# The second mixer's opening: products on the unscaled stream, keys and ctx norm behind them

## The chip, the cores and the metric

The kernel runs on one core of a Trainium2 chip. The metric is the device time of one execution in microseconds (us). The engines are PE (matrix products), DVE and ACT (element by element), POOL, and SP, whose queue issues most of the DMAs.

## The reference

A network of two blocks at batch 1, on 512 tokens of width 1024. The first block has two mixer layers; the first of them also updates a context of 256 tokens, which the second one reads for keys and values. The lines that matter:

```python
h = rms_norm(x, norm_g) * (1 + scale[:, None]) + shift[:, None]
hc = rms_norm(ctx, norm_g) * (1 + scale_c) + shift_c
p = h @ w_in                    # a_in, b_in (pool), q, k, v, gate
pkv = hc @ w_in[:, K_OFF:G_OFF] # layer 1: keys and values of the context
y = jnp.concatenate([fourier_mix(a_in, w_fourier), pool_mix(b_in, w_pool, pool_scale), attn], axis=-1)
x_new = x + gate[:, None] * ((y * jax.nn.silu(g)) @ w_out)
```

`scale`, `shift` and `gate` are products of one vector with large matrices (the modulations). The second block has, twice, a hybrid mixer (a retention and an HGRN2 part, a gate, an out projection) and a convolutional feed-forward part, each with modulations of its own.

## The kernel before

Activations lie transposed: a tile is 128 features by 512 tokens, eight tiles make the stream `x`, and ctx tiles have 256 columns. Each operand is kept as a high and a low part: a weight tile of 128x1024 is split by ACT (`wh`, L151) and DVE (`wl`, L152), and each product is three matmuls (L178 to L180, where 512 tokens of the activations move; L201 to L203 for keys and values, where the activations are loaded and 256 columns of the weight move). A product of one weight tile with all eight tiles of the stream is thus 24 matmuls of 512 columns. Weights are streamed through two buffers by SP in the order of the array `w_in`, whose column tiles the host lays out in the order of use.

A list scheduler sets the order of every engine, except in `pinned(...)` stretches, where the written order stands. PE, DVE, ACT and POOL each run their order strictly. Background work, the modulations of later layers, is handed to the scheduler by `background(n)`: `n` steps, each a DMA of 256 KB into one of two buffers `gr` and a product on DVE with a broadcast vector `cb` (`gemv`, L515). `background(99)` takes what is left; `mod_finish` and `gain` (L519 to L525) then make the modulation usable. A new vector `cb` is itself a DMA, three ACT steps and a DVE product (`bcast_silu`, L500).

The places that are spoken of below:

- **The junction of mixer 0 and mixer 1** (about 405 to 480 us). Before, `cross_first` (L415) handles it: the last two tiles of the out projection are made in halves of 256 tokens, so that the norm of the first half can begin early; the norm (`norm_mix`, L269) is shared by DVE, ACT and POOL, and PE's first products of mixer 1 are the keys of both halves and a pool projection on the normed stream. The context's norm follows, on the same engines.
- **The other junctions** use `cross` (L305). PE goes on with three products on A*x, the stream times the modulation's gain but without the division by the norm ("deferred" tiles). Meanwhile the norm's factor r is found (a statistic on PE, `rstd` on ACT and DVE). A deferred tile is finished by `z(j)`: its sum in PSUM times r, plus a bias, which PE makes from the shift vector (`bias_rows` L309, `bias_cols`, `bias_pick`). `first(k)` and `second(k)` (L374, L378) make the normed stream for all later products: DVE multiplies by gain and r, ACT adds the shift and writes `hh`, DVE writes the low part `hl`.
- **Mixer 1's tail** (about 655 to 680 us): the last attention head, the gates, and then the out projection.
- **The first hybrid mixer's end** (about 860 to 1005 us), called ssm0: four retention heads, eight gate tiles (product on PE, silu, product with `y` L1621, split into `y2h` and `y2l`), and the out projection, whose residual is L1054.

Of the kernel before, what the change touches and what calls it, by code (L numbers as in the profile page):

```python
# [12 lines left out]
F32 = mybir.dt.float32  # L13
# [7 lines left out]
P = 128  # L21
# [15 lines left out]
def tile_model(ctx: ExitStack, tc: tile.TileContext, a: dict, out: bass.AP, dbg=None):  # L37
# [191 lines left out]
    def stat_add(i, xk, k, sl, eng=None, late=None):  # L229
        n = sl.stop - sl.start  # L230
        if k == 0:
            acc[i] = sb("acc", [P, T], F32, 1, cp) if i == 0 else sb("acc2", [P, C], F32, 1, sub[0])
            act(acc[i][:, sl], xk[:, sl], AF.Square)
            return None
# [70 lines left out]
    def cross(load, steps, res, per, hs, A, sh, swap=None):  # L305
        d0 = wi[0] + KT * per
        b = {}

        def bias_rows(j):  # L309
            if not b:  # L310
                b["pick"] = tmp("rs", 1)
                V.tensor_reduce(out=b["pick"], in_=ident.rearrange("p (g c) -> p c g", g=4)[:, 0:1], op=ALU.add, axis=AX.X)
                b["sh"] = tmp("t", KT * 32).rearrange("p (k c) -> p k c", c=32)
# [8 lines left out]
        def bias_cols():  # L322
            rows = tmp("t", ND * P)
            act(rows, b["ps"][:, :ND * P], AF.Copy)
            b["rows"] = rows

        def bias_pick():
            o = b["ps"][:, ND * P:ND * P + ND]
            for j in range(ND):
                PE.matmul(o[:, j:j + 1], b["rows"][:, j * P:(j + 1) * P], b["pick"], start=True, stop=True, skip_group_check=True)  # L330
            b["col"] = tmp("rs", ND)
# [8 lines left out]
        for m in range(KT - 1):  # L340
# [4 lines left out]
            pre(m)  # L345
        with pinned(PE_, DVE_, ACT_, POOL_):
# [6 lines left out]
            bias_rows(2)  # L353
            bias_cols()
            run(st[-4:])
            bias_pick()
            last = res(m, o, ALL)
            pre(m)
            V.tensor_tensor(out=acc[0], in0=acc[0], in1=last, op=ALU.add)
            if swap is not None:  # L360
                swap()
            zs, ts, os_ = [], {}, []

            def defer(n):
                w = next_w(n)
                os_.append(pt("g"))
                return gemm_steps(os_[-1], w, hs)

            def z(j):
                zs.append(tmp("t"))  # L370
# [3 lines left out]
            def first(k):  # L374
                ts[k] = tmp("ta" if k % 4 < 3 else "t")
# [6 lines left out]

            st = defer(2)
            run(st[:5])
            sq = pt("m")
            PE.matmul(sq, ones, acc[0], start=True, stop=True)
            run(st[5:])
            r = rstd(sq, T, 1.0 / D, "ta", tmp("t"))
            run(defer(1))
# [8 lines left out]
            first(3)  # L398
            second(1)
            z(1)  # L400
# [10 lines left out]
            z(2)  # L411
        anchor.update(tails(DVE_, ACT_))
        return zs

    def cross_first(load, steps, res, full, stat_c, hs, hc, mods_, k_steps, p_steps, weights):  # L415
        (Ax, mx), (Ac, mc) = mods_
        for m in range(KT - 2):
            w = load(m, 2)
            o = pt("g")
            run(steps(o, w, ALL))  # L420
            res(m, o, ALL)
            full(m, w)
        with pinned(PE_, DVE_, ACT_, POOL_):
            tail = [(m, load(m, KT - m), pt("g")) for m in range(KT - 2, KT)]
            for m, w, o in tail:
                run(steps(o, w, HA))
                last = res(m, o, HA)
            sq = pt("m", C)
            stat(sq, acc[0][:, HA], True)
            rest = [f for m, w, o in tail for f in steps(o, w, HB)]  # L430
            run(rest[:3])
            stat(sq, last, False)
            ra = stat_rstd(sq)
            run(rest[3:])
            lasts, adds, halves, rs_ = [], [], [], {}

            def res_b(j):
                m, w, o = tail[j]
                lasts.append(res(m, o, HB, adds))

            def take():
                halves.clear()
                W.load(wi[0] + 2)
                W.split(wi[0] + 1, halves)
                if halves:
                    halves[0]()
                weights.append(next_w(0))

            def late_half():
                if len(halves) > 1:  # L450
                    halves[1]()

            def stat_b():
# [1407 lines left out]
```

## Time and profile before

| | |
|---|---|
| median of 3 runs | 2064.59 us (2062.36 to 2070.71) |
| profiled execution | 2064.29 us, its span 2062.5 us, mean granted PE clock 0.993 |
| busy | PE 2007.8 us (97%), DVE 1418.3 (69%), ACT 945.2 (46%), POOL 120.1 (6%) |
| weight splits | DVE 338.4 us in 279 instructions, ACT 291.0 us |
| background products (L515) | DVE 208.9 us in 304 instructions |

Times in the rows are counted from the start of the span; 1.79 us of the execution lie outside it. PE's records overlap (a 512-column matmul shows 0.39 us but the next starts 0.23 us later), so its pace is read from starts. The granted clock (PEclk) is a share of 2.4 GHz.

### The profile page before, as it was taken

How to read it: one execution, taken by the hardware profiler on the slowest of the kernel's cores; microseconds unless marked ns; L12 is line 12 of the kernel's file. 1: busy time of each engine (PE TensorE's matmuls, PEld its weight loads, DVE VectorE, ACT ScalarE, POOL GpSimd, SP SyncE). 2: the span in 40 equal slices, each digit the busy share in tenths (PEclk: the TensorE clock that was granted, in tenths of full speed). 3: DMA queues.
4: the chain of work that ended last, by engine and by line, in shares of the span. 5: the costliest groups of instructions: out<-in, count | busy, mean ns of one | idle time of the engine just before them, and what ended most of it. 6: DMA issues, size and time to landing. Idle time of an engine off the chain costs nothing. (4 is left out here: it accounts for less than half of the span.)

```text
span 2062.5 us, 30076 instructions
## 1 busy us (share of the span) xinstructions
PE 2007.8 (97%) x11398; PEld 1718.6 (83%) x11398; DVE 1418.3 (69%) x2722; ACT 945.2 (46%) x1629; POOL 120.1 (6%) x129
## 2 busy tenths in 40 slices
PE   7999999989999999999999999999999999999997
PEld 4988988889898888888788888878988888888887
DVE  4879997686676688888787776338986667444323
ACT  4527487253547455435453333225643645333322
POOL 2101010130101100000100000000000010000010
PEclk9999999999999999999999999999999999999999
DMA  8342325724012332355446665323122223333332
GB/s 295 108 148 63 116 64 157 244 79 150 22 52 67 118 112 72 103 173 181 159 149 214 207 208 181 99 88 101 52 72 82 82 84 104 101 92 102 88 101 77
DMA packets 96129, 245.92 MB, mean 119 GB/s; under 512 B 12592, under 2 KB 17952, under 8 KB 95728
## 3 DMA queue, kind: packets, MB, share of 16 engines
q1 hardware_dynamic: 94752, 242.90, 37.3%
q8 instruction: 90, 1.47, 0.3%
q0 software_dynamic: 656, 0.57, 0.1%
q10 hardware_dynamic: 576, 0.52, 0.1%
q14 instruction: 55, 0.45, 0.1%
HBM read 239.76 MB, written 4.19 MB: 118 GB/s over the span
## 5 line engine op out<-in xcount | busy, mean ns | idle before, releaser
L152 DVE TENSOR_TENSOR wl<-wr,wh 128x1024 fp32r<-128x1024 f32 (+1 forms) x279 | 338.4, 1213 | 238.2 <-ACT wh L151 234.9
L178 PE MATMUL g<-hh,wh 128*128 128x512 f32 (+1 forms) x1256 | 493.1, 393 | 0.0
L180 PE MATMUL g<-hh,wl 128*128 128x512 f32 (+1 forms) x1256 | 491.1, 392 | 1.3 <-DVE wl L152 1.1
L179 PE MATMUL g<-hl,wh 128*128 128x512 f32 (+1 forms) x1256 | 492.0, 392 | 0.0
L151 ACT ACTIVATE wh<-wr 128x1024 fp32r<-128x1024 f32 (+1 forms) x279 | 291.0, 1043 | 384.9 <-PE g L179 302.7
L515 DVE SCALAR_TENSOR_TENSOR gs<-gr,cb 128x512 bf16<-128x512 f32 x304 | 208.9, 687 | 99.6 <-DMA gr<-ada_w 80.0
L180 PEld LDWEIGHTS g<-hh,wl 128*128 128x128 f32 x1256 | 236.2, 188 | 47.6 <-DVE wl L152 1.3
L179 PEld LDWEIGHTS g<-hl,wh 128*128 128x128 f32 x1256 | 236.5, 188 | 47.1 <-DVE hl L381 1.2
L178 PEld LDWEIGHTS g<-hh,wh 128*128 128x128 f32 x1256 | 236.5, 188 | 45.8 <-issue 1.0
L201 PE MATMUL g<-wh,hh 128*128 128x256 f32 x704 | 203.6, 290 | 3.6 <-ACT hh L661 3.1
L202 PE MATMUL g<-wl,hh 128*128 128x256 f32 x704 | 203.9, 290 | 2.3 <-DVE wl L152 2.3
L203 PE MATMUL g<-wh,hl 128*128 128x256 f32 x704 | 202.7, 289 | 2.2 <-DVE hl L295 2.1
L201 PEld LDWEIGHTS g<-wh,hh 128*128 128x128 f32 x704 | 136.6, 194 | 6.9 <-ACT hh L661 3.4
L178 PE MATMUL g<-g2h,wh 128*128 128x512 f32 (+1 forms) x374 | 141.9, 379 | 0.0
L179 PE MATMUL g<-g2l,wh 128*128 128x512 f32 (+1 forms) x374 | 141.5, 378 | 0.0
L180 PE MATMUL g<-g2h,wl 128*128 128x512 f32 (+1 forms) x374 | 141.5, 378 | 0.0
L203 PEld LDWEIGHTS g<-wh,hl 128*128 128x128 f32 x704 | 136.7, 194 | 4.0 <-DVE hl L295 2.6
L202 PEld LDWEIGHTS g<-wl,hh 128*128 128x128 f32 x704 | 136.7, 194 | 3.4 <-DVE wl L152 2.5
L241 POOL TENSOR_TENSOR acc<-acc,ta 128x512 f32<-128x512 f32 (+1 forms) x28 | 39.7, 1420 | 1405.0 <-ACT ta L236 1404.8
L1664 ACT ACTIVATE t<-t,k_conv_b 128x512 f32<-128x512 f32 x44 | 31.8, 723 | 166.3 <-DVE t L1662 166.3
L178 PEld LDWEIGHTS g<-g2h,wh 128*128 128x128 f32 x374 | 70.7, 189 | 13.7 <-issue 0.4
L180 PEld LDWEIGHTS g<-g2h,wl 128*128 128x128 f32 x374 | 70.8, 189 | 13.0
(430 smaller groups left out, 3578.0 us busy)
## 6 DMA issues: line engine op xcount, KB each, us to landing
wr<-w_in SPq DMA_DIRECT2D x112, 512.0 KB, 3.5
gr<-ada_w SPq DMA_DIRECT2D x192, 256.0 KB, 3.2
wr<-w_gate SPq DMA_DIRECT2D x44, 512.0 KB, 3.6
wr<-w_val SPq DMA_DIRECT2D x44, 512.0 KB, 3.7
gr<-w_mod SPq DMA_DIRECT2D x64, 256.0 KB, 2.9
wr<-w_out SPq DMA_DIRECT2D x32, 512.0 KB, 3.6
wr<-w_down SPq DMA_DIRECT2D x32, 512.0 KB, 3.5
raw<-w_mod_n SPq DMA_DIRECT2D x16, 512.0 KB, 8.4
```

The lines of the kernel that those rows point to most:

```text
L151: act(hi[:, :k], raw[:, :k], AF.Copy)
L152: V.tensor_tensor(out=lo[:, :k], in0=raw[:, :k], in1=r32(hi[:, :k]), op=ALU.subtract)
L178: PE.matmul(o, whi, xhi, start=start, stop=False)
L179: PE.matmul(o, whi, xlo, start=False, stop=False)
L180: PE.matmul(o, wlo, xhi, start=False, stop=stop)
L201: PE.matmul(ob, xh[:, sl], whi[:, k], start=fst, stop=False, skip_group_check=True)
L202: PE.matmul(ob, xh[:, sl], wlo[:, k], start=False, stop=False, skip_group_check=True)
L203: PE.matmul(ob, xl[:, sl], whi[:, k], start=False, stop=lst, skip_group_check=True)
L241: add()
L515: V.scalar_tensor_tensor(out=s, in0=t, scalar=1.0, in1=cb, op0=ALU.mult, op1=ALU.mult, accum_out=dst[:, i, m:m + 1])
L1664: last_silu = act(cv, cv, AF.Silu, bias=cvb[:, l, f:f + 1])
```

## The change

- `cross` is used for the junction of the two mixers too, with four deferred tiles: pool projections 2 and 3 and gates 2 and 3 (`nd=4`). The first two sums lie in PSUM tag `s`, the other two in `g`. `cross_first` is gone, and with it the halves of 256 tokens and POOL's share of the norm.
- The context's norm (`ctx_norm`) is written into the same pinned stretch, in three groups of 2, 3 and 3 tiles, on DVE and ACT, ahead of the stream's `second(k)`.
- Keys come after the deferred tiles; the order of layer 1's weights in `w_in` follows. The two pools and the two gate products with `y` are done from the finished deferred tiles.
- Bias rows of the deferred tiles are made later, except at the junction into ssm0.
- The small copies of the Fourier weight (`cw`) move from DVE to ACT.
- Background: 4, 4, 2, 2 steps around the attention of each mixer in place of 8 each, 6 per gate tile for 4; in ssm, 6 per retention head for 4, and 2 for only the first four gate tiles in place of all eight.

```diff
-    def cross(load, steps, res, per, hs, A, sh, swap=None):
+    def cross(load, steps, res, per, hs, A, sh, swap=None, nd=3, post=None, ctx_norm=None):
...
             def defer(n):
                 w = next_w(n)
-                os_.append(pt("g"))
+                os_.append(pt("s" if first_stage and len(os_) < 2 else "g"))
...
+            if first_stage:
+                normc = ctx_norm()
             first(0)
             first(1)
-            run(defer(0))
+            run(defer(nd - 3))
             z(0)
-            W.load(wi[0] + 2)
-            W.split(wi[0] + 1)
-            first(2)
+            if nd == 3:
+                next_split()
+                first(2)
+            else:
+                normc[0]()
+                first(2)
+                first(3)
+                normc[1]()
+                z(1)
+                run(defer(0))
+                normc[2]()
+                z(2)
+                next_split()
             second(0)
...
             second(7)
-            z(2)
+            z(nd - 1)
...
-                V.tensor_copy(cw[rows, j * P + 64 * g:j * P + 64 * g + 64], pw[rows, j * 64:j * 64 + 64])
+                act(cw[rows, j * P + 64 * g:j * P + 64 * g + 64], pw[rows, j * 64:j * 64 + 64], AF.Copy)
...
+            def go(ks):
+                for k in ks:
+                    (hh, hl), t = hc[k], tmp("tf", C)
+                    V.scalar_tensor_tensor(out=t, in0=xc[k], scalar=gc[:, k:k + 1], in1=rc, op0=ALU.mult, op1=ALU.mult)
+                    act(hh, t, AF.Identity, bias=new[1][:, k:k + 1])
+                    V.scalar_tensor_tensor(out=hl, in0=t, scalar=new[1][:, k:k + 1], in1=r32(hh), op0=ALU.add, op1=ALU.subtract)
+            return [partial(go, ks) for ks in (range(0, 2), range(2, 5), range(5, 8))]
...
-            background(4)
+            background(6)
...
-            background(2)
+            if m < 4:
+                background(2)
```

The order of instructions shows what this does at three places. First DVE at the junction, before: the factor of the second token half (`rn_5025`), a weight split, then that half's norm (`hl` low part of the stream, made from `ta` and `tf`), with the factor of the context (`rn_5109`) after the second tile.

```order
L219 SCALAR_TENSOR_TENSOR rn_5025<-ta_5026,rn_5025 128x256
L152 TENSOR_TENSOR wl_5034<-wr_5011,wh_5035 128x1024
L290 SCALAR_TENSOR_TENSOR ta_5038<-y_4186,gain_4180,rn_5025 128x256
L290 SCALAR_TENSOR_TENSOR tf_5041<-y_4293,gain_4180,rn_5025 128x256
L295 SCALAR_TENSOR_TENSOR hl_4149<-ta_5038,mod_1457,hh_4148 128x256
L290 SCALAR_TENSOR_TENSOR ta_5051<-y_4388,gain_4180,rn_5025 128x256
L295 SCALAR_TENSOR_TENSOR hl_4151<-tf_5041,mod_1457,hh_4150 128x256
L217 SCALAR_TENSOR_TENSOR ta_5110<-m_5106,rn_5109 128x256
L218 SCALAR_TENSOR_TENSOR ta_5110<-ta_5110,rn_5109 128x256
L219 SCALAR_TENSOR_TENSOR rn_5109<-ta_5110,rn_5109 128x256
```

And the change at the same place: the context's factor `rn_5060`, two tiles' first halves (`ta`), the first deferred tile times r (`e_5096`, which is `z(0)`), and then the context's tiles, L1276 and L1278 in turn.

```order
L219 SCALAR_TENSOR_TENSOR rn_5060<-ta_5061,rn_5060 128x256
L385 SCALAR_TENSOR_TENSOR ta_5067<-y_4186,gain_4180,tk_5003 128x512
L385 SCALAR_TENSOR_TENSOR ta_5069<-y_4295,gain_4180,tk_5003 128x512
L380 TENSOR_TENSOR e_5096<-s_4968,tk_5003 128x512
L1276 SCALAR_TENSOR_TENSOR tf_5099<-yc_4289,gain_4182,rn_5060 128x256
L1278 SCALAR_TENSOR_TENSOR cl_4165<-tf_5099,modc_1458,ch_4164 128x256
L1276 SCALAR_TENSOR_TENSOR tf_5103<-yc_4385,gain_4182,rn_5060 128x256
L1278 SCALAR_TENSOR_TENSOR cl_4167<-tf_5103,modc_1458,ch_4166 128x256
L385 SCALAR_TENSOR_TENSOR ta_5107<-y_4392,gain_4180,tk_5003 128x512
L385 SCALAR_TENSOR_TENSOR tk_5109<-y_4503,gain_4180,tk_5003 128x512
L1276 SCALAR_TENSOR_TENSOR tf_5111<-yc_4496,gain_4182,rn_5060 128x256
L1278 SCALAR_TENSOR_TENSOR cl_4169<-tf_5111,modc_1458,ch_4168 128x256
```

What moved: the eight context tiles, L1276 and L1278 each, now stand ahead of every `hl` of the stream, and each L1278 reads what ACT makes (`ch`) from the L1276 right before it.

Second, PE at the junction, before: the context's part of the last out tile (`ych`), the statistic of the second half, and the first matmuls of the keys of the first half (`g_5055`).

```order
L179 MATMUL g_4979<-ycl_4137,wh_4715 128x256
L180 MATMUL g_4979<-ych_4136,wl_4714 128x256
L264 MATMUL m_5022<-acc_4257,ones 128x256
L264 MATMUL m_5022<-ta_4929,ones 128x256
L201 MATMUL g_5055<-wh_4786,hh_4148 128x256
L202 MATMUL g_5055<-wl_4785,hh_4148 128x256
L203 MATMUL g_5055<-wh_4786,hl_4149 128x256
```

And the change: the end of the fourth deferred tile (`g_5126`, gate 3) and the first key matmuls (into `g_5296` and `g_5297`), which need `hh` of the stream and the weight `wh_5169`, `wl_5168`.

```order
L178 MATMUL g_5126<-hh_4162,wh_5013 128x512
L179 MATMUL g_5126<-hl_4163,wh_5013 128x512
L180 MATMUL g_5126<-hh_4162,wl_5012 128x512
L201 MATMUL g_5296<-wh_5169,hh_4148 128x256
L201 MATMUL g_5297<-wh_5169,hh_4148 128x256
L202 MATMUL g_5296<-wl_5168,hh_4148 128x256
L202 MATMUL g_5297<-wl_5168,hh_4148 128x256
L203 MATMUL g_5296<-wh_5169,hl_4149 128x256
```

What moved: four products of 24 matmuls on A*x stand between the last out tile and the keys, and the keys now need the norm of all 512 tokens at once.

Third, DVE at the end of ssm0's gates, before: gemv steps (L515) between and behind the last gate tile's operations (`tg_10654`, `y2l_10677`).

```order
L515 SCALAR_TENSOR_TENSOR gs_10555,mod_6_91<-gr_10553,cb_4405 128x512
L1453 TENSOR_TENSOR tg_10654<-g_10629,tg_10654 128x512
L1621 TENSOR_TENSOR tg_10654<-y_1649_8217,tg_10654 128x512
L515 SCALAR_TENSOR_TENSOR gs_10559,mod_6_91<-gr_10557,cb_4412 128x512
L224 TENSOR_TENSOR y2l_10677<-tg_10654,y2h_10676 128x512
L515 SCALAR_TENSOR_TENSOR gs_10604,mod_6_91<-gr_10602,cb_4405 128x512
L152 TENSOR_TENSOR wl_10738<-wr_10700,wh_10739 128x1024
L515 SCALAR_TENSOR_TENSOR gs_10608,mod_6_91<-gr_10606,cb_4412 128x512
```

And the change:

```order
L152 TENSOR_TENSOR wl_10643<-wr_10580,wh_10644 128x1024
L1425 TENSOR_TENSOR tg_10611<-g_10586,tg_10611 128x512
L475 TENSOR_TENSOR cb_11132<-cb_11132,gr_11134 128x512
L1594 TENSOR_TENSOR tg_10611<-y_1645_8158,tg_10611 128x512
L475 TENSOR_TENSOR cb_11139<-cb_11139,gr_11141 128x512
L224 TENSOR_TENSOR y2l_10618<-tg_10611,y2h_10617 128x512
L1022 SCALAR_TENSOR_TENSOR y_7651<-g_10647,mod_6_91,y_7651 128x512
L152 TENSOR_TENSOR wl_10679<-wr_10641,wh_10680 128x1024
```

What moved: all gemv steps of this batch stand ahead of these rows, none stands behind the last `y2l`, and two L475 products of the next batch's vector `cb` have come in ahead of it.

## Rows read from the trace of the kernel before

**Rows 1.** Stretches: us, busy PE, PEld, DVE, ACT, POOL, PEclk, DMA share, GB/s.

```profile
427.00:480.00 53.00, 46.89 (x343) 44.07 (x342) 47.36 (x100) 29.38 (x57) 15.02 (x17) 0.94 0.35 110
700.00:760.00 60.00, 58.68 (x343) 49.06 (x342) 44.37 (x73) 29.00 (x43) 3.84 (x3) 1.00 0.42 134
```

**Rows 2.** PE's waits at the junction (427 to 480): total us, times, longest.

```profile
PE g L202 <- DVE wl L152: 2.3, 1, 2.3
PE g L203 <- DVE hl L295: 2.1, 2, 1.9
```

**Rows 3.** Stretches of 1 us behind the wait at 441.5; PEclk after POOL.

```profile
442.00:443.00 1.00, 1.00 (x8) 0.98 (x7) 1.00 (x4) 0.97 (x3) 0.21 (x1) 0.68 1.01 412
...
445.00:446.00 1.00, 1.00 (x7) 1.00 (x7) 1.00 (x3) 0.51 (x1) 1.00 (x2) 0.61 0.00 0
```

**Rows 4.** PE's waits from 480 to 540, columns as in rows 2.

```profile
PE m L960 <- DVE cw L965: 1.0, 1, 1.0
```

**Rows 5.** PE's waits from 900 to 1010, columns as in rows 2.

```profile
PE g L178 <- ACT y2h L223: 2.8, 1, 2.8
PE g L178 <- DVE y L1054: 1.2, 1, 1.2
```

**Rows 6.** DVE in ssm0: start, us, engine, line, out<-in (timeline).

```profile
983.26 0.68 DVE L1453 TENSOR_TENSOR tg<-g,tg 128x512 f32<-128x512 f32 x1
...
985.36 0.69 DVE L224 TENSOR_TENSOR y2l<-tg,y2h 128x512 fp32r<-128x512 f32 x1
...
1003.79 2.72 DVE L1054 SCALAR_TENSOR_TENSOR y<-g,mod,y 128x512 f32<-128x512 f32 x4
```

**Rows 7.** DVE's waits from 866 to 985.4, columns as in rows 2.

```profile
DVE gs L515 <- DMA gr<-ada_w: 6.1, 8, 3.3
DVE sd L1422 <- PE m L180: 3.0, 2, 1.8
```

**Rows 8.** Timeline of PE in the key products: two rows 24 matmuls apart.

```profile
436.00 0.28 PE L201 MATMUL g<-wh,hh 128*128 128x256 f32 x1
...
438.88 0.28 PE L201 MATMUL g<-wh,hh 128*128 128x256 f32 x1
```

**Rows 9.** Timeline of PE with 512 columns: two rows 24 matmuls apart.

```profile
974.76 0.39 PE L180 MATMUL g<-hh,wl 128*128 128x512 f32 x1
...
980.20 0.39 PE L180 MATMUL g<-y2h,wl 128*128 128x512 f32 x1
```

**Rows 10.** Timeline of PE: the bias rows of one deferred tile.

```profile
713.41 0.64 PE L319 MATMUL m<-wr,t 128*32 128x128 f32 x16
```

**Rows 11.** Timeline at the junction: ACT, DVE, POOL in rstd and ctx norm.

```profile
438.37 0.46 ACT L214 ACTIVATE ta<-m,eps_c 128x256 f32<-128x256 f32 x1
...
440.23 0.42 DVE L219 SCALAR_TENSOR_TENSOR rn<-ta,rn 128x256 f32<-128x256 f32 x1
...
446.62 2.79 POOL L274 TENSOR_TENSOR tf<-yc,rn 128x256 f32<-128x256 f32 x3
...
446.96 0.96 DVE L290 SCALAR_TENSOR_TENSOR ta<-yc,gain,rn 128x256 f32<-128x256 f32 x1
...
449.32 0.47 DVE L290 SCALAR_TENSOR_TENSOR tf<-yc,gain,rn 128x256 f32<-128x256 f32 x1
...
449.83 0.51 ACT L291 ACTIVATE ch<-tf,modc 128x256 fp32r<-128x256 f32 x1 [1.37 <-DVE tf L290]
```

**Rows 12.** Page, part 5: the weight split on ACT (busy, mean ns, idle).

```profile
L151 ACT ACTIVATE wh<-wr 128x1024 fp32r<-128x1024 f32 (+1 forms) x279 | 291.0, 1043 | 384.9 <-PE g L179 302.7
```

**Rows 13.** Timeline of DVE in the next junction: first halves of a norm.

```profile
735.08 1.42 DVE L376 SCALAR_TENSOR_TENSOR ta<-y,gain,t 128x512 f32<-128x512 f32 x2
```

**Rows 14.** Timeline of PE and DVE at the last attention head of mixer 1.

```profile
664.46 0.63 PE L949 MATMUL m<-c_ident,ta 128*128 128x128 f32 x4
...
668.17 0.69 DVE L224 TENSOR_TENSOR yl<-y,yh 128x512 fp32r<-128x512 f32 x1 [0.70 <-ACT yh L223]
```

**Rows 15.** Background products on DVE from 860 to 1004: ns min/median/max.

```profile
L515 DVE SCALAR_TENSOR_TENSOR gs<-gr,cb x56: 678/689/694, 866.0 to 1002.5; 128x512 bf16<-128x512 f32 x56
```

More of the change, by code (lines that the diff above doesn't have):

```diff
@@ L345, in cross @@
             pre(m)
+            if post is not None:
+                post(m, w)
         with pinned(PE_, DVE_, ACT_, POOL_):
@@ L410, in cross @@
             second(7)
-            z(2)
+            z(nd - 1)
         anchor.update(tails(DVE_, ACT_))
         return zs
[L415 to L453, printed above, removed]
-                sq = pt("m", C)
-                stat(sq, acc[0][:, HB], True)
-                stat(sq, lasts[-1], False)
-                rs_["b"] = stat_rstd(sq)
-            def c_part():
-                run(k_steps(HA, 0))
-                run(p_steps(HA))
-                sq = pt("m", C)
-                stat_c(sq)
-                rs_["c"] = stat_rstd(sq)
-            weights.append(next_w(0))
-            def take_whole():
-                W.load(wi[0] + 2)
-                W.split(wi[0] + 1)
-                weights.append(next_w(0))
-            norm_mix(hs, x, Ax, mx, HA, ra, {("second", 0): lambda: res_b(0), ("second", 1): lambda: res_b(1),
-                                             ("second", 2): lambda: run(adds), ("second", 4): lambda: full(*tail[0][:2]),
-                                             ("mixed_act", 6): lambda: full(*tail[1][:2]), ("pool_sub", 6): lambda: (take(), late_half()),
-                                             ("pool_sub", 7): stat_b})
-            take_whole()
-            norm_mix(hs, x, Ax, mx, HB, rs_["b"], {("second", 1): c_part})
-            for f in (k_steps(HA, 1), k_steps(HB, 0), k_steps(HB, 1), p_steps(HB)):
-                run(f)
-            norm_mix(hc, xc, Ac, mc, HA, rs_["c"], {})
-        anchor.update(tails(DVE_, ACT_))
@@ L1151, in pools_ @@
                 pool(oc, C, l, c, pw, yc[2 + c])
+        if l == 1:
+            for c in range(2):
+                pool(zs[c], T, l, c, pool_w(l, c), y[2 + c])
+                gate_mul(zs[2 + c], T, y[2 + c])
+            rope_tables(l)
         def gates(m):
@@ L1175, in kqv @@
                 os_, oc = tok()
-                done()
+                if done is not None:
+                    done()
                 kx = qk_lat(os_, l, 1)
@@ L1216, in mixer @@
         four()
-        background(8)
+        background(4)
         done = att(0, 4, kq)
-        pools_(1, done)
-        background(8)
+        if l == 0:
+            pools_(1, done)
+        else:
+            gates(0)
+            done()
+        background(4)
         done = att(1, 4, kq)
         kq = kqv(1, done)
-        background(8)
+        background(2)
         done = att(0, 6, kq)
-        gates(0)
+        if l == 0:
+            gates(0)
         done()
         gates(1)
-        background(8)
+        background(2)
         done = att(1, 6, kq)
         open_sub(f"out{l}")
-        for m in range(2, 8):
+        for m in range(2 + 2 * l, 8):
             gates(m)
-            if m == 2:
+            if m == 2 + 2 * l:
                 done()
-            background(4)
+            background(6)
         background(99)
@@ L1601, in ssm_layer @@
             q = (q, *parts(q))
-            background(4)
+            background(6)
             w = next_w()
```

98 lines of the change are left out of this document (54 added, 44 removed).

## The prediction

> **What bounds the kernel now.** I read the share of busy time first: PE is busy 2007.8 of 2062.5 us, so about 55 us of the span are PE's waits, and a change can only gain those, PE's own work, or time at a lowered clock. The table of stretches says where they lie. Between 427 and 480 us, the junction that is rewritten, PE is busy 46.89 of 53 us, and its granted clock is 0.94 [rows 1]. The list of PE's waits names the releasers there: a weight's low part (2.3 us) and the low parts of the normed stream (longest 1.9) [rows 2]; the rest of the 6.1 us is in short waits. The clock is the second price of a wait. After the 1.9 us wait that ends at 441.5 the 1 us stretches show 0.68, then 0.50 twice (1.2 GHz, the lower level), then 0.61, and full speed after [rows 3]: 0.32 + 0.5 + 0.5 + 0.39 = 1.7 us lost. The 2.3 us wait is followed by the same pattern. So the junction loses 6.1 + 3.4 = 9.5 us.
>
> Two other places matter. From 480 to 540 PE waits once, 1.0 us, for the `cw` copies on DVE [rows 4]. In ssm0 it waits 2.8 us for the high part of the last gate tile and 1.2 us for the out projection's residual [rows 5]. The timeline shows why: the last gate tile's sum was ready at 977.0 (the row at 980.20 is the fifteenth matmul of the out projection behind it [rows 9]), but DVE reaches its L1453 at 983.26 and its `y2l` at 985.36 [rows 6]. DVE is some 6 us behind. Eight gemv steps follow that row, so the residual L1054, which needs the finished modulation, comes at 1003.79 only [rows 6]. DVE itself had waited, in the stretch before, 6.1 us for gemv DMAs and 3.0 us for PE [rows 7]; only the latter is slack for certain.
>
> **The change part by part.** *PE's work.* The halves go: 96 + 48 matmuls of 256 columns become 48 + 24 of 512. Twenty-four of 256 take 2.88 us [rows 8], twenty-four of 512 take 5.44 [rows 9], so 17.28 becomes 16.32 us: -1.0. Bias rows for four tiles come in, 0.64 us each [rows 10]: +2.6. The four picks cost about as much as one of those, +0.6. The statistics, 14 of 256 columns before and 10 of 256 and one of 512 now, give back perhaps 0.2. Sum +2.0 us (bounds +1.5 and +3). The Trainium skill (TensorE: Matmul & The Clock Gate, Back-to-back issue gap) gives a fixed 2.5 ns per matmul beside the columns, by which the 72 matmuls fewer would save 0.2 us and not 1.0, and the sum be +2.8; the rows' 120 ns and 227 ns decide here.
>
> *The junction.* I count from t = 0, where PE starts the first deferred tile, the point that is 427 us before. Four tiles are 21.8 us [rows 9]; with two bias rows, the picks and the statistics PE is through at about 25, and no tile waits, since A*x needs no norm. The context's statistic ends at about 13.9 in this. Its factor takes 2.3 us from ACT's first row to DVE's last [rows 11], so it is there at 16.4; DVE works strictly in order, and the stream's `first(0)` stands behind it. Two first halves take 1.42 us [rows 13], `z(0)` 0.7: 18.5. Then the context. DVE's L1276 (0.47 us), ACT 0.51 after its start, ACT's own 0.51, and DVE's L1278 behind it: 0.51 + 0.51 + 0.02 + 0.39 (issue to issue) = 1.43 us per tile, since each L1278 waits for ACT and the next L1276 stands behind it [rows 11]. Eight are 11.4 us; two more first halves 1.4 and `z(1)` 0.7 lie between: 32.0. After `z(2)` (0.7) ACT has that tile's bias (0.7), the weight split (1.04) [rows 12] and `hh` of tile 0 (0.7): 35.1. PE's first key matmul needs that `hh` and that weight. So PE stands from 25 to 35, **10 us**. Then it is paced: eight `hl` and four `first` at 0.71 [rows 13] keep DVE until about 44, and the third sum's place in PSUM is only free after `z(3)`, at 44.7; PE has 50 matmuls (6.0 us) in these 9.7 us: **3.7 us** more. With one fall of the clock, 1.7, the junction loses 15.4 us against 9.5 before: **+5.9**. Bounds: -9.5 if nothing stalls, +9 if the clock stays at its lower level through the paced keys and after.
>
> That takes 0.47 us for L1276. Before, the same operation took 0.96 us where POOL was at work on its part of the norm (446.62 for 2.79 us), and 0.47 behind it [rows 11]; in the new order POOL has only two small DMA issues here. At 0.96 the chain would be 7.8 us longer. (The Trainium skill, SBUF — State Buffer, Who interferes with whom, says that a DVE instruction with two SBUF inputs contends with a POOL instruction that reads SBUF, which fits these rows; by it the 0.47 holds.)
>
> The pool weights' loads stay on POOL's queue, earlier and with nothing ahead of them; the rope tables' loads go to SP behind the same weights as before, and DVE's four rope products stand ahead of the stream's factor, where DVE has waited for ACT anyway. Both cost nothing as long as the loads land within those 8 us; otherwise all of the above moves by the delay.
>
> *`cw` on ACT:* the 1.0 us wait goes [rows 4], **-1.0** (0 if ACT's queue delays it as long; ACT is busy 46%).
>
> *Mixer 1's tail.* From the last head's transposes (664.46) to its last low part (668.17 and 0.69) are 4.4 us [rows 14]. Before, two whole gate tiles followed, 10.9 us; now two gates fewer are left, and some 16 matmuls (3.6 us) stand between. **+0.7** (0 to +2.5).
>
> *ssm0.* Ahead of the last `y2l` DVE now has eight gemvs more, at 0.69 and 0.08 for the accumulator [rows 15]: 6.2 us; two L475 at 0.7, and `mod_finish`, `gain` and a copy at about 1.0: 8.6 us in all. Against it stand the 3.0 us of waits for PE [rows 7] and about 1 us of short hand-offs into which the new order puts gemvs. So the last tile is 4.6 us later. PE has six matmuls more (1.4 us) to do before it needs it, and the 1.2 us wait for the residual goes, since nothing follows `y2l`: 4.6 - 1.4 - 1.2 = 2.0. I take **+1.5**, because fewer gemvs (19 for 21) stand in the gates themselves; bounds -4 (both waits gone) and +6 (8.6 - 1.4 - 1.2, no slack). More gemvs in the same time also ask more of two `gr` buffers, which DVE waited for already; SP's queue holds weights behind them.
>
> The other groups of background move work that the scheduler spreads over stretches in which DVE, 69% busy, has room. The moved bias rows at the other junctions change no count. Both: 0.
>
> **Sum:** 2.0 + 5.9 - 1.0 + 0.7 + 1.5 = +9.1 us. The profiled execution took 2064.29, 0.3 below the median of 2064.59; so **2073.4 us**. A measurement here can tell about 0.5%, 10.3 us: the line runs at 2054.3 and 2074.9.
>
> **Rivals.** *The junction runs dry no more* (chance 0.13). For it: at the next junction, where `cross` is used already, PE is busy 58.68 of 60 us [rows 1]. Against: nothing stands there between `z(0)` and the second halves. Pipelined over ACT and DVE the eight context tiles would take 8 x 0.78 = 6.2 us, 5.2 less, half of the wait; they must not bind at all. Then 2.0 - 9.5 - 1.0 + 0.7 and ssm0 at -4: 2052.5 us.
>
> *A stall for a stall* (0.22): PE waits for the stream's `hh` as long as it did for `hl` and the weight, the change moves the loss and gains nothing: 2.0 + 0 - 1.0 + 0.7 + 1.5 = +3.2, 2067.5 us. My ladder has 10 us of wait; it would have to be 4 us too long.
>
> *DVE is late in ssm0* (0.25), the slower side: no slack takes up the eight gemvs, or the `gr` DMAs come slower than they are asked for and DVE waits in order; ssm0 costs +6, and the whole 2.0 + 5.9 - 1.0 + 0.7 + 6 = +13.6, 2077.9 us. It decides from +3.0 in ssm0, where the sum passes 2074.9; that is `y2l` later by more than 5.6 us.
>
> **How the numbers follow.** My forecast has 0.35, of which 0.25 within 0.5% and 0.10 above, for its own spread of some 3 us (2069 to 2077) reaches over the line. Another 0.05 is for what I do not see. Faster 0.13; within 0.5%: 0.22 + 0.25 + 0.03 = 0.50; slower 0.25 + 0.10 + 0.02 = 0.37. The range, 2055 to 2080 us, leaves out the dry-free case below and the far end of the late DVE above.
>
> **What would show it.** Right: a wait of PE of some 10 us for `hh` or `hl` of the stream right behind the fourth deferred tile, a second of a few us for the place of the keys' third sum, a granted clock of 0.50 behind; no wait for `cw`, none for the residual in ssm0; a wait for the last `y2h` of 5 us or so. Wrong: eight context tiles in much less than 11 us on DVE, PE going from gate 3 into the keys with 2 us or less; ssm0's gates without a wait.

## The result and the profile after

The changed kernel takes 2079.76 us (2077.30 to 2081.26, 4 runs), against 2064.55 us for the kernel before on the same chip: a ratio of 1.0076, interval 1.0062 to 1.0090, or +15.2 us. The profiled execution is the fastest of the four, 2077.30 us, with a span of 2075.5 us. PE's and DVE's busy times hardly differ from before: the span grew by 13.0 us, PE's busy time by 4.1.

```profile
PE 2011.9 (97%) x11392; PEld 1715.2 (83%) x11392; DVE 1423.5 (69%) x2714; ACT 950.6 (46%) x1640; POOL 104.5 (5%) x110
```

To place the 13 us, I cut the span at PE's first and last matmuls of the out projections (times of starts, from the timelines of PE). "mixer 0 out" ends with the context's last out matmul, and "junction + mixer 1" with mixer 1's first out matmul. "ssm0" reaches to the end of its out projection; "rest" is from there to PE's last matmul; the 10 us behind that one are left out.

| us | to mixer 0 out | mixer 0 out | junction + mixer 1 | mixer 1 out | ssm0 | rest |
|---|---|---|---|---|---|---|
| before | 357.9 | 69.0 | 253.5 | 45.7 | 302.5 | 1023.8 |
| after | 357.6 | 70.0 | 259.1 | 46.1 | 305.9 | 1027.0 |
| difference | -0.4 | +1.0 | **+5.6** | +0.4 | **+3.4** | **+3.2** |

The list of PE's waits (us in total, times, longest) names the large one, and it is new:

```profile
PE g L201 <- ACT hh L389: 11.2, 3, 10.5
...
PE m L178 <- ACT uh L223: 3.9, 4, 2.4
PE m L928 <- DMA fw<-w_fourier: 3.9, 2, 2.6
...
PE g L178 <- ACT y2h L223: 2.1, 1, 2.1
...
PE m L1399 <- DVE sd L1394: 1.6, 2, 1.4
PE g L179 <- DVE yl L224: 1.5, 1, 1.5
...
PE m L399 <- DVE acc L365: 0.6, 3, 0.3
PE g L201 <- DVE dt L380: 0.5, 1, 0.5
```

**The junction.** In PE's timeline the 10.5 us stand between the last deferred tile and the first key matmul, and 0.48 us for the place of the third key sum stand behind:

```profile
464.45 0.80 PE L201 MATMUL g<-wh,hh 128*128 128x256 f32 x2 [10.50 <-ACT hh L389]
473.81 0.39 PE L201 MATMUL g<-wh,ch 128*128 128x256 f32 x1 [0.48 <-DVE dt L380]
```

DVE's timeline shows why. The stream's own factor is there, but DVE stands 6.35 us in its written order for the context's factor. Then each context tile runs through DVE, ACT and DVE alone: from 451.67 to 453.13 is 1.46 us a tile, and only 0.96 of it is DVE's work.

```profile
444.02 0.42 DVE L217 SCALAR_TENSOR_TENSOR ta<-g,rn 128x256 f32<-128x256 f32 x1 [6.35 <-ACT rn L216]
...
447.21 0.47 DVE L1276 SCALAR_TENSOR_TENSOR tf<-yc,gain,rn 128x256 f32<-128x256 f32 x1
...
451.67 0.48 DVE L1276 SCALAR_TENSOR_TENSOR tf<-yc,gain,rn 128x256 f32<-128x256 f32 x1
452.73 0.49 DVE L1278 SCALAR_TENSOR_TENSOR cl<-tf,modc,ch 128x256 fp32r<-128x256 f32 x1 [0.58 <-ACT ch L1277]
453.13 0.48 DVE L1276 SCALAR_TENSOR_TENSOR tf<-yc,gain,rn 128x256 f32<-128x256 f32 x1
...
461.40 0.69 DVE L380 TENSOR_TENSOR e<-g,tk 128x512 f32<-128x512 f32 x1
```

The clock follows the wait. In stretches of 1 us (PEclk behind POOL's busy time), where the kernel before had four low ones after its wait, two of them at 0.50 [rows 3], it stays at 0.50 (1.2 GHz) from before the first key matmul until 469:

```profile
464.00:465.00 1.00, 0.55 (x2) 0.50 (x2) 1.00 (x2) 1.00 (x3) 0.00 (x0) 0.50 0.00 0
...
468.00:469.00 1.00, 1.00 (x7) 1.00 (x6) 1.00 (x2) 1.00 (x3) 0.00 (x0) 0.50 0.99 400
469.00:470.00 1.00, 1.00 (x8) 1.00 (x7) 1.00 (x3) 1.00 (x3) 0.00 (x0) 0.67 0.23 91
470.00:471.00 1.00, 1.00 (x10) 1.00 (x10) 1.00 (x2) 1.00 (x3) 0.00 (x0) 1.00 0.06 16
```

From 464.45 on, 4.55 us at half speed and one at 0.67 cost 2.3 + 0.3 = 2.6 us.

**ssm0.** The wait for the residual [rows 5] is gone, and that for `y2h` went from 2.8 to 2.1 us. But PE now waits in the retention heads, 3.3 us for `uh` (1.3 before) and 1.6 for `sd`. PE's waits from 860 to 1030 us, before and after:

```profile
PE m L178 <- ACT uh L223: 1.3, 2, 0.6
...
PE m L178 <- ACT uh L223: 3.3, 2, 2.4
```

DVE's own waits (866 to 998 us) show what made DVE late there: the gemv DMAs. Ahead of the last `y2l` they cost 6.1 us in [rows 7] and now

```profile
DVE gs L483 <- DMA gr<-ada_w: 11.2, 12, 2.0
```

These waits did not grow, they moved. Before, gemvs also stood behind the last `y2l`, where no gate tile waits for them, and over the whole batch (860 to 1020 us) DVE waited as long:

```profile
DVE gs L515 <- DMA gr<-ada_w: 11.5, 12, 3.3
```

Up to the last `ul`, that is in the retention heads, it is 6.5 us now and was 1.9. Counted from mixer 1's last out matmul, the last `y2l` comes 6.7 us later than before.

**The bias rows.** In each of the three junctions behind ssm0 PE's dense run is now broken twice by 16 small matmuls, and the statistic waits, where before one block of 32 stood ahead of it. PE at the end of ssm1's out projection, before and then after:

```profile
1683.93 1.08 PE L319 MATMUL m<-wr,t 128*32 128x128 f32 x32
...
1696.49 0.64 PE L322 MATMUL m<-wr,t 128*32 128x128 f32 x16
1703.69 1.12 PE L399 MATMUL m<-acc,ones 128*128 128x512 f32 x2 [0.17 <-DVE acc L365]
1708.19 0.64 PE L322 MATMUL m<-wr,t 128*32 128x128 f32 x16
```

### The profile page after: what moved, and what is told of

It reads as the page before. It is cut to its first block, busy times and chain, and to the rows that moved or that the text cites. A ratio compares the mean times of both kernels' runs of the same rounds, so it can differ in the third digit from the quotient of the medians.

```text
span 2075.5 us, 30041 instructions
## 1 busy us (share of the span) xinstructions
PE 2011.9 (97%) x11392; PEld 1715.2 (83%) x11392; DVE 1423.5 (69%) x2714; ACT 950.6 (46%) x1640; POOL 104.5 (5%) x110
## 5 line engine op out<-in xcount | busy, mean ns | idle before, releaser
L178 PE MATMUL g<-hh,wh 128*128 128x512 f32 x1232 | 485.6, 395 | 0.0
L180 PE MATMUL g<-hh,wl 128*128 128x512 f32 x1232 | 484.1, 393 | 1.4 <-DVE wl L152 1.4
L179 PE MATMUL g<-hl,wh 128*128 128x512 f32 x1232 | 484.6, 394 | 0.0
L179 PEld LDWEIGHTS g<-hl,wh 128*128 128x128 f32 x1232 | 232.0, 188 | 46.7 <-issue 1.0
L180 PEld LDWEIGHTS g<-hh,wl 128*128 128x128 f32 x1232 | 231.7, 188 | 47.0 <-DVE wl L152 1.6
L178 PEld LDWEIGHTS g<-hh,wh 128*128 128x128 f32 x1232 | 232.0, 188 | 45.7 <-issue 1.6
L241 POOL TENSOR_TENSOR acc<-acc,ta 128x512 f32<-128x512 f32 x24 | 36.0, 1502 | 1382.7 <-ACT ta L236 1382.7
L179 PEld LDWEIGHTS g<-g2l,wh 128*128 128x128 f32 x374 | 70.8, 189 | 13.1
```

Of the source, the lines that this page charges most:

```text
L178: PE.matmul(o, whi, xhi, start=start, stop=False)
L179: PE.matmul(o, whi, xlo, start=False, stop=False)
L180: PE.matmul(o, wlo, xhi, start=False, stop=stop)
L241: add()
```

## The experiments

There are two theories. **Mine:** three separate costs, DVE's ladder over the context tiles at the junction, the bigger ssm groups, and the broken bias rows. **The rival for the junction:** order and hand-offs are not the limit; DVE's amount of work at mixer 1's opening is, and a wait taken away in one place comes back in another. Kernels measured together share the runs of the kernel before; where not said otherwise an edit is made to the changed kernel.

Runs of one kernel scatter by up to 10 us (last section), so medians of four to six runs do not tell 3 us apart. I read the segments of the profiled runs first, and use medians where a dozen runs stand behind them. Segments scatter too, and not alike: junction + mixer 1 takes 258.4 to 259.2 us in the five traces that leave that stretch as it is in the changed kernel (the changed kernel, e3, e4, e7, e14), but ssm0 takes 302.4 to 307.5 in the ten traces with its larger groups.

**e1, the context's norm last.** The three groups go behind the last `z`.

```diff
-                normc[0]()
                 first(2)
...
             z(nd - 1)
+            if first_stage:
+                for f in normc:
+                    f()
```

> The change, with the context's norm moved behind the stream's: the eight L1276/L1278 pairs stand behind the last z. If the 10.5 us wait for hh comes from these pairs standing ahead of the stream's second halves (my theory), DVE reaches the first hl about 11 us earlier and the wait goes to 1 us or less, the paced keys behind it shrink too, and the time falls by 12 to 16 us, to about 2065. Rival: the wait belongs to deferring as such (factor, z, weight split, hh in a row, whatever the context does); then 7 us or more of it stay and the time stays above 2074.

Measured: 2075.13 us (2068.91 to 2079.10), ratio 1.0049 (1.0029 to 1.0069). PE's wait for `hh` there is gone, as expected, but junction + mixer 1 came to 255.4 us, only 3.7 less. PE's waits from 427 to 500 us say where the rest went:

```profile
PE m L1010 <- ACT kl L828: 3.7, 1, 3.7
PE g L201 <- ACT ch L1277: 2.1, 1, 2.1
```

The stall moved to the context's own tiles and, at the pool's product L1010, to a row of the keys' preparation (`kl`). First point for the rival.

**e2, the groups pipelined.** In a group all L1276 and ACT rows are written first, then all low parts.

```diff
+                ts = {k: tmp("tf", C) for k in ks}
                 for k in ks:
-                    (hh, hl), t = hc[k], tmp("tf", C)
...
+                for k in ks:
+                    hh, hl = hc[k]
...
```

> The change, with the context's norm in its place but written in groups: first all L1276 of a group of 2, 3 and 3 tiles, then all its low parts, so that DVE does not wait for ACT in every tile. If the chain DVE, ACT, DVE of 1.45 us per tile is what makes the 10.5 us, the eight tiles take 6 to 7 us on DVE in place of 11.4, and the wait for hh falls to 5 to 6.5 us; time about 2073 to 2075. Rival: the wait ends with something else (the weight split on ACT, the z of the third tile, the pool operations put between); then it falls by less than 2 us.

Measured: 2076.26 us (2068.82 to 2078.92), ratio 1.0061 (1.0040 to 1.0082). The wait for `hh` is 5.2 us, and the segment 253.5 us, 5.6 less and equal to before; e5, with the same edit at the junction, has 253.5 too. The ladder's hand-offs are shown to cost that much. DVE still stands 6.6 us for the context's factor, and from then on it hardly pauses: it is busy 35.3 of the 36 us from 446 to 482.

**e3, ssm background back to 4 and 2 for all tiles.**

```diff
-            background(6)
+            background(4)
...
-            if m < 4:
-                background(2)
+            background(2)
```

> The change, with the background groups of the two hybrid mixers as before (4 per retention head, 2 for each of the eight gate tiles). If eight more gemvs ahead of the last gate tile make DVE late (the waits for uh of 2.4 and 1.0 us and for sd of 1.4 us in the retention), the stretch from the first out projection of mixer 1 to the end of ssm0 goes back by 3 to 4 us: time about 2076. Rival: these waits come from the later start or from DMA, not from the number of gemvs; then the time stays at 2079 to 2080.

Measured: 2076.41 us (2076.07 to 2079.07), ratio 1.0067 (1.0049 to 1.0085). ssm0 takes 300.8 us, 5.1 less, and 298.4 to 300.8 in the four traces with the old groups (e3, e5, e10, e12), below all ten with the larger ones. The segment behind it gives 1.9 back in this trace (244.6 for 242.7 us to ffn0's down projection), but e14, without this edit, has 245.2 there, so that this is within its scatter. In PE's waits from 860 to 1030 us `uh` is back at its 1.3, and the residual's wait has returned:

```profile
PE g L178 <- DVE y L1022: 2.7, 1, 2.7
PE m L178 <- ACT uh L223: 1.3, 2, 0.6
```

**e4, bias rows early at every later junction.**

```diff
-        early = swap is not None and not first_stage
+        early = not first_stage
```

> The change, with the bias rows and picks of the other three junctions at their old places (last out tile) again. The trace shows each extra break in a row of 512-column products at about 0.35 us in and out, and 0.8 us more per junction. Theory: 3 junctions give back 2.4 us in all, time about 2077.4. Rival: the 0.8 us per junction is the next junction's own scatter; then no change.

Measured: 2077.40 us (2075.37 to 2078.94), ratio 1.0067 (1.0052 to 1.0083). The rest is 1022.4 us, 4.6 less. One part of it hardly scatters: from ssm1's out projection to ffn1's down projection it is 241.6 us in all six traces with early rows (the kernel before, e4, e5, e8, e10, e12) and 242.6 or 242.7 in all ten with late ones, so this junction costs 1.1 us. At ssm1's out projection the block is whole again, and the statistic no longer waits:

```profile
1695.25 1.08 PE L322 MATMUL m<-wr,t 128*32 128x128 f32 x32
...
1703.24 1.02 PE L399 MATMUL m<-acc,ones 128*128 128x512 f32 x2
```

**e5, the three together.** The edits of e2, e3 and e4.

> The change with three things mended at once: the context's norm in groups (as in e2), the background sizes of the hybrid mixers of before (e3), the old places of the bias rows at the other three junctions (e4). By the stretches of the three traces they are worth 5.6, 3.2 and 4.6 us in different places, so if the causes are separate they add up: 13 us less than the change, about 2066, the time of before. If two of them share a cause, or one only moved a wait into another's stretch, the sum is 9 us or less and the time stays above 2070.

Measured: 2067.53 us (2065.03 to 2071.10, 12 runs), ratio 1.0018 (1.0007 to 1.0030): the edits add up to about 12 us, and 3.6 us over the kernel before remain.

**e6, half of the context behind the stream.** Tiles 0 to 3 before the stream's `second(k)`, 4 to 7 behind, each pipelined.

```diff
-                normc[2]()
...
             z(nd - 1)
+            if first_stage:
+                normc[2]()
...
-            ... (range(0, 2), range(2, 5), range(5, 8))]
+            ... (range(0, 2), range(2, 4), range(4, 8))]
```

> The change, with the context's norm in groups, tiles 0 to 3 where they were and tiles 4 to 7 behind the stream's norm. With all eight behind (e1) the wait of PE for hh went, but the opening of mixer 1 only became 3.7 us shorter, since DVE's work was still to be done and PE waited for it elsewhere; with groups (e2), which take DVE's own idle time away, 5.6. Theory: DVE is the bound of this opening, so only its idle time can be won; moving half of the context behind gains little over e2, 0 to 2 us, time 2071 to 2075. Rival: the order decides, and each tile behind the stream is worth its 0.8 us; then 3 us or more below e2.

Measured: 2075.84 us (2073.67 to 2080.04), ratio 1.0061 (1.0039 to 1.0083). The wait for `hh` is 2.2 us, but the segment 254.4 us, no better than e2: a key weight's low part is now late.

```profile
PE g L202 <- DVE wl L152: 2.5, 1, 2.5
PE g L201 <- ACT hh L389: 2.2, 1, 2.2
```

**e7, the mixers' background back.** 8 around each half of the attention, 4 per gate.

```diff
-        background(4)
+        background(8)
         done = att(0, 4, kq)
...
-            background(6)
+            background(4)
```

> The change, with the background groups of the two first mixers as before (8 around each attention step, 4 per gate tile). In the change PE waits 1.5 us for a low part at the start of mixer 0's out projection, where it waited 0.6 before, and that stretch is 1 to 3.7 us longer. Theory: six gemvs per gate tile make DVE late there; with four it goes back to 69 us and the time falls by 1 to 3 us. Rival: it is the bias row and the full-width out tiles that lengthen it; then no change.

Measured: 2081.02 us (2075.40 to 2084.76), ratio 1.0081 (1.0056 to 1.0106). A miss: mixer 0's out stretch is not shorter but 73.5 us, at the upper end of what the other traces with `cw` on ACT have (70.0 to 73.4).

**e8, the kernel before with the new ssm background alone.**

```diff
-            background(4)
+            background(6)
...
-            background(2)
+            if m < 4:
+                background(2)
```

> The kernel before, with only the new background sizes of the hybrid mixers (6 per retention head, 2 for four of the eight gate tiles). If these alone make DVE late in ssm0, the stretch from the end of mixer 1 to the end of ssm0's feed-forward products becomes about 3 us longer than before, with waits for uh above 2 us: time about 2066. If the loss needs the rest of the change, the time is that of before.

Measured: 2067.86 us (2061.93 to 2072.41, 10 runs), ratio 1.0016 (0.9999 to 1.0033); ssm0 308.4 us, 5.9 more than before. The retention is where it is lost (PE's waits, 860 to 1030 us):

```profile
PE m L178 <- ACT uh L223: 5.4, 2, 2.8
PE g L178 <- ACT y2h L223: 3.1, 1, 3.1
PE m L1427 <- DVE sd L1422: 1.3, 1, 1.3
```

**e9 and e10, the stream first.** DVE's 6.35 idle us (the expectation says 6.75) invite an order in which the stream's norm comes first, then the `z`, then the context (pipelined); e10 adds the edits of e3 and e4. In both, the stream's new tiles are written ahead of the fourth deferred product, which still reads A*x from the same buffers: gate 3 is computed from other operands.

```diff
             else:
-                normc[0]()
+                second(0)
                 first(2)
+                second(1)
...
                 run(defer(0))
...
```

> In the changed kernel, and in the two runs that moved or regrouped the context's norm, DVE stands 6.75 us in its written order for the context's factor at the junction, with the stream's first(0) behind it, though the stream's own factor is there. Here the stream's eight tiles (first and second) come first, then the four z, and the context's factor and its eight tiles (in groups, as in the pipelined run) last. Theory, the idle 6.75 us of DVE in order is what is left of the wait for hh: PE's wait for hh of the stream is under 1 us, the clock does not fall there, no other wait of more than 1.5 us appears up to 500 us, the segment junction + mixer 1 is 245 to 249 us (259.1 in the changed kernel, 253.5 with pipelined groups), time about 2067 to 2070 us. Rival, the amount of DVE's work bounds the opening: the wait comes back at the context's ch or at a pool's low part as it did with the context last, the segment stays at 253 or more, time 2074 to 2077 us.

> The same order at the junction, with the ssm background back to 4 and 2 and the bias rows early at the other junctions. If the effects add up as in the run with three edits: 2058 to 2062 us by the theory, 2 to 6 us below the kernel before; by the rival (DVE's work is the bound) 2066 to 2069 us, no better than that run.

Measured: e9 2074.76 us (2069.90 to 2077.49), ratio 1.0051 (1.0035 to 1.0066), segment 252.5 us; e10 2066.23 us (2065.18 to 2070.80, 11 runs), ratio 1.0018 (1.0009 to 1.0028), segment 253.3. PE has no wait for `hh` left, but one of 4.7 us for a place in PSUM that `z` frees. DVE's idle time was not filled either: the low parts now wait for ACT's `hh` (e9).

```profile
445.40 0.75 DVE L390 SCALAR_TENSOR_TENSOR hl<-ta,mod,hh 128x512 fp32r<-128x512 f32 x1 [5.65 <-ACT hh L389]
```

**e11 and e12, to fill the idle time.** Here no `second(k)` stands before the last deferred product. Four `first` and two `z` are put into DVE's idle time; then come the context's factor and five tiles, `z(2)`, the key weight, four `second`, three context tiles, and the rest. e12 adds e3 and e4.

```diff
             else:
-                normc[0]()
                 first(2)
                 first(3)
+                z(0)
+                z(1)
+                normc[0]()
                 normc[1]()
-                z(1)
                 run(defer(0))
-                normc[2]()
                 z(2)
                 next_split()
...
```

> The run before this one wrote the stream's norm over the tiles that the fourth deferred product still reads (its output is that of other operands), and PE's wait came back in another form, 4.7 us for the place in PSUM that the z rows free. Here no second(k) stands ahead of the last deferred product. In the 6.75 us in which DVE stood in order (for the context's factor) it makes first(0) to first(3) and z(0), z(1); then come the context's factor and five of its tiles, z(2), the key weight, second(0) to second(3), the other three context tiles, z(3), and the rest. Only the order of DVE and ACT at this junction differs from the pipelined run. Theory, what was left of the wait was DVE's idle time in its written order: the wait for hh falls from 5.2 us (pipelined) and 10.5 (changed kernel) to under 1.5, no wait for a z above 1 us, junction + mixer 1 at 245 to 249 us, time 2068 to 2072 us. Rival, DVE's amount of work bounds the opening: the wait appears further on (context's ch, a pool's kl) and the segment stays at 253 us or more, time 2074 to 2077 us.

> The same order, with the ssm background back to 4 and 2 and the bias rows early at the other junctions, as in the run with three edits (2067.5 us). Theory: 2059 to 2063 us, 1 to 5 us below the kernel before on the same chip. Rival: 2066 to 2069 us.

Measured: e11 2074.77 us (2073.52 to 2078.96), ratio 1.0057 (1.0044 to 1.0070), segment 255.5 us; e12 2070.88 us (2064.54 to 2076.18, 12 runs), ratio 1.0034 (1.0022 to 1.0046), segment 255.2. The segment is no shorter than in e2. The wait for `hh` shrank to 2.1 us, and PE waits later for the first keys' rotation:

```profile
PE g L201 <- DVE tk L803: 4.5, 1, 4.5
PE g L201 <- ACT hh L389: 2.1, 1, 2.1
```

DVE gets to that row at 479.65, behind the rest of the norm, weight splits, and the pool's work; from the factor on (447.6 to 480.4) it is busy 30.4 of 32.8 us. But this does not settle my theory of the idle time, because that time stayed. The third `first` writes the last of three buffers `ta`, which PE's statistic of the context still reads, and waits for it; and the factor comes later, since ACT's rows of two `z` now stand ahead of it. DVE in e11:

```profile
443.32 0.75 DVE L385 SCALAR_TENSOR_TENSOR ta<-y,gain,tk 128x512 f32<-128x512 f32 x1 [4.17 <-PE g L264]
...
447.61 0.42 DVE L217 SCALAR_TENSOR_TENSOR tf<-g,rn 128x256 f32<-128x256 f32 x1 [1.68 <-ACT rn L216]
```

That is 5.85 us idle for 6.35 in the changed kernel. DVE stands some 6 us at this place in every order here; what a filled stretch would bring was not tried.

**e13, less work for DVE.** As e11, against which the edit is shown, but the eight L1276 are left out: ACT and the low part read the context without its norm and gain.

```diff
-                    V.scalar_tensor_tensor(out=ts[k], in0=xc[k], ...
-                    act(hc[k][0], ts[k], ...
+                    act(hc[k][0], xc[k], ...
```

> As the run that filled DVE's idle time (e11_fill), but the context's norm leaves out its division by the norm and its gain: ACT and the low part read the context tile directly, so eight DVE instructions of 0.43 us in a row, 3.4 us, are gone and nothing else is moved. Theory, DVE's amount of work bounds mixer 1's opening: PE's wait for the rotated keys (tk, 4.5 us) and the one for hh (2.1 us) together fall by 2.5 to 4 us, and junction + mixer 1 from 255.5 to 251 to 253 us. Rival, hand-offs between DVE and ACT and the places in PSUM set it, whatever the work: the two waits stay within 1 us of 6.6, the segment at 254.5 to 256.5 us.

Measured: 2071.22 us (2068.87 to 2073.58), ratio 1.0038 (1.0023 to 1.0053). The segment is 251.8 us, 3.7 less than e11 for 3.4 us less of DVE's work; the two waits are 4.5 us together, 2.1 less (a little under the 2.5 to 4 expected), and PE's mean clock from 427.6 to 500 us is 0.98 for 0.95. So the work that DVE has behind the context's factor sets the opening, as the rival has it. Hand-offs hardly explain it, for in e11 the low parts of the context wait only 0.2 us for ACT. That no order can help is not shown: work moved into DVE's idle time would leave that stretch just as well.

```profile
PE g L201 <- DVE tf L1020: 2.9, 1, 2.9
PE g L201 <- ACT hh L389: 1.6, 1, 1.6
```

**e14, `cw` back on DVE.**

```diff
-                act(cw[rows, ...], pw[rows, ...], AF.Copy)
+                V.tensor_copy(cw[rows, ...], pw[rows, ...])
```

> The changed kernel with only the small Fourier weight copies (cw) back on DVE. Prediction's step: the 1.0 us wait for cw comes back, time +1. Rival, the wait for the DMA of fw ends last there (1.3 us), so the copies' engine decides nothing: no wait for cw beyond that, wait at that product between 1 and 2 us, the segment junction + mixer 1 within 1 us of 259.1, time within the scatter of 2079.8 us.

Measured: 2074.77 us (2072.85 to 2077.09, 4 runs), ratio 1.0053 (1.0037 to 1.0070). Mixer 1's segment is 259.2 us, 0.1 more. With the copies on ACT that product waits 1.3 us for a DMA; back on DVE it waits as long for the copy:

```profile
PE m L928 <- DVE cw L933: 1.4, 1, 1.4
```

So there the edit decides nothing. But mixer 0's out stretch is 68.2 us instead of 70.0, and the wait for `yl` is gone. In the changed kernel's DVE timeline a background gemv that waits for its DMA stands ahead of the last head's row L1019, which `yh` and `yl` need:

```profile
360.23 0.69 DVE L483 SCALAR_TENSOR_TENSOR gs<-gr,cb 128x512 bf16<-128x512 f32 x1 [2.07 <-DMA gr<-ada_w]
...
360.85 0.69 DVE L1019 TENSOR_TENSOR y<-y,tf 128x512 f32<-128x512 f32 x1
```

In e14 the scheduler put no gemv there. That the edit reached this place only through the scheduler's order is read from one pair of traces. The stretch is 68.1 to 69.0 us in the three traces with `cw` on DVE (the kernel before, e8, e14) and 70.0 to 73.5 in the thirteen with it on ACT.

No version here beats the kernel before; of those with the new junction the nearest, e5 and e10 (e10 with other operands in gate 3), take 0.18% more.

## Why the prediction was right or wrong

The time lay in the range, 6.4 us above the forecast; the direction given most was wrong. It came out slower by 0.76%, and I had given that 0.37.

- **The wait at the junction, 10 us:** right in place, cause and size: 10.5 us behind the fourth deferred tile, for `hh`, with 1.46 us a context tile for 1.43. The next term was not: 3.7 us for paced keys measured 0.5, since the lower clock slowed PE (2.6 us lost for 1.7) while DVE caught up. Waits and clock make 10.5 + 0.5 + 2.6 = 13.6 us for 15.4. With PE's added work, `cw` and the tail the prediction had +7.6 us from mixer 0's out to mixer 1's; the three segments show +7.0. The rivals "runs dry no more" and "a stall for a stall" are excluded by the wait itself. Two figures of that working are off without moving the sum: 13.9 + 2.3 is 16.2, not 16.4, and eight L1276 of 0.96 us would add 3.9 us; it takes the eight L1278 as well to add 7.8.
- **What I did not see there:** the hand-offs are only half of it. Pipelining gains 5.6 us (e2); four other orders (e1, e6, e11, and e9 with other operands) end between 252.5 and 255.5 us, and e11 with 3.4 us less of DVE's work ends 3.7 us lower (e13, 251.8). DVE is full behind the context's factor; its idle 6 us ahead of it are in all these orders, and whether they can be used stays open. The share of the norm that POOL had [rows 11] is now DVE's and ACT's. The 0.47 us taken for L1276 held (0.47 and 0.48 above), with POOL busy 2.1 of 72 us from 427.6 on; the Trainium skill (SBUF — State Buffer, Who interferes with whom) says that a DVE instruction with two SBUF inputs contends with a POOL instruction that reads SBUF, and the trace agrees.
- **`cw`, -1.0:** a miss. The DMA of the Fourier weight is right behind the copy, and PE waits 1.3 us for it. The bound "0 if ACT's queue delays it" had the value, not the reason.
- **ssm0, +1.5:** the mechanism (more gemvs than slack) was right, the term mis-sized at +3.4 us (302.4 to 307.5 in ten traces against 302.5, so this is good to some 3 us), and the place wrong. I expected a wait of 5 us for the last `y2h`; it fell to 2.1. PE loses the time in the retention heads, where six gemvs a head wait in order for their DMAs, 6.5 us for 1.9; over the whole batch these waits are as long as before. The prediction's own sign for the rival "DVE is late in ssm0", a `y2l` later by more than 5.6 us, came true with 6.7. The sentence that more gemvs "also ask more of two `gr` buffers" was in the text without a price in the sum. Alone on the kernel before the edit costs 5.9 us in ssm0 (e8); in the changed kernel taking it back gains 5.1 there (e3).
- **"The moved bias rows at the other junctions change no count. Both: 0":** this is the step that failed. The count is the same, but two breaks of the dense stream instead of one, and a statistic that has lost its cover, cost +3.2 us over the rest of the kernel; undone, 4.6 us come back there (e4; about 1.1 of it in ffn0's down projection, where other runs scatter as much). Of one junction 1.1 us are sure, since ten traces and six agree on it (e4). How they divide between the break and the statistic was not tried.
- **The other background, set at 0 as well:** mixer 0's out stretch became 1.0 us longer, 1.6 to 4.5 in the other variants with `cw` on ACT. Restoring the mixers' counts did not help (e7). With `cw` back on DVE it is 1.8 us shorter than in the changed kernel, and one gemv stands elsewhere (e14); that this gemv is the cause is argued.
- **The sum and the sign:** 9.1 as forecast, 3.2 from the bias rows and 1.9 more in ssm0, less 0.6 in the three segments around the junction and 0.4 ahead of them, make 13.2 us; the profiled run grew by 13.0, for 0.2 us behind PE's last matmul were gained. The other 2.2 of the +15.2 us come from the choice of the profiled run, which is the fastest of its four. So the prediction failed by its small terms: those set at 0 or +1.5 carried the time over the line; the chance of slower should have been larger than that of no change.

## What to carry to other kernels

In an order that is written by hand, count for each tile the whole chain DVE, ACT, DVE, and write all first halves of a group ahead of all second halves. Then look at the engine behind the wait: where it is full, another order of the same rows only moves the wait to the next product (e1, e6, e11). What is left is less work, or idle time ahead of that stretch; and when an order is meant to fill idle time, check in the trace that it did. Background work that waits for its DMA in an in-order engine costs what is queued behind it, so a bigger group must be priced at each place where it stands. And "the same count" of small matmuls is not the same time when they break a dense run twice.

## What the runs showed of the hardware that I had not expected

- Runs of one kernel on one core differ by up to 10 us with the mean granted clock: e1 took 2068.91 us at 0.994 and 2079.10 at 0.990; the kernel before, measured together with it, 2058.85 at 0.996 and 2067.30 at 0.991. The segment up to mixer 0's out, about 357 us, took between 355.3 and 362.1 us in the sixteen profiled runs, though hardly an edit reaches it. What sets the clock there was not tried.
- The clock stayed at 0.50 for 4.5 us and more after PE had begun to work again at 464.45; full speed came back after 5.2 us, and after 3.8 to 4.7 us in the four other traces with the same 10.5 us wait (e3, e4, e7, e14). After the 1.9 us wait of the kernel before it had come back within some 4 us [rows 3]: a wait five times as long took little more clock with it.
- A wait of some 2 us did not always lower the clock. After the 1.9 and the 2.3 us wait of the kernel before it fell, after one wait each of 2.1 to 2.5 us in e1, e6, e8 and e11 it stayed at full speed.
